# Hybrid attention and mLSTM step: the first group's output projection joins the last scan, the other groups' mLSTM halves join their attention halves, and w_out is held as float16 pairs

## The chip, the cores and the metric

One core of one Trainium2 chip runs the kernel. The metric is the device time of one execution in microseconds (us), as the median of the runs shown. The engines are named as in the profile: PE (TensorE matmul), PEld (its weight loads), DVE (VectorE), ACT (ScalarE), POOL (GpSimd), SP (the queue that issues most transfers).

## The reference

One layer: adaLN modulations from the conditioning, an input projection, attention beside a bidirectional mLSTM, one output projection over both, then a SwiGLU feed-forward layer. All inputs and outputs are float32.

```python
h = rmsnorm(x, norm1_w) * (1 + sc1) + sh1
aq, ak, av, mq, mk, mv, mo, mg = jnp.split(h @ w_in, SPLIT_POINTS, axis=-1)
...
attn_o = attention(aq, keys, vals)
...
hm, st_f, st_b = mlstm_bidir(heads(mq), heads(mk) * (MLSTM_DK ** -0.5), heads(mv), gates, init_f, init_b)
hm = rmsnorm(hm.transpose(0, 2, 1, 3), mlstm_norm_w.reshape(MLSTM_HEADS, MLSTM_DV))
hm = (hm.reshape(B, T, MLSTM_WIDTH) * jax.nn.sigmoid(mo.astype(F32))).astype(x.dtype)
mix = jnp.concatenate([attn_o, hm], axis=-1) @ w_out
x = x + g1 * mix
h2 = rmsnorm(x, norm2_w) * (1 + sc2) + sh2
x = x + g2 * swiglu(h2, w_gu, w_down)
```

D_MODEL is 1024, the attention and mLSTM widths are 512 each, D_FF is 2816. There are 128 context tokens and 1024 latent tokens, so 1152 rows.

## The kernel before

The 1152 rows are nine blocks of 128 (`NB`), block 0 the context, in three groups of three blocks (`CB`, `CT` = 384 columns). Float32 accuracy is kept by splitting every operand into a high and a low part and adding three products: high by high, high by low, low by high. The parts are fp32r (feed-forward, scores, output projection) or float16 (input projection, attention values).

The stages, in the order of the program:

1. Front: modulations from `w_ada` (`ada_rest`, L417, whose units load 512 KB and issue eight `strip_products`), normalisation, keys, values and gates, then queries. Four chunks of the modulations are made here; the sixth (`ns` = 5, the second gate) is left for stage 3.
2. Projection of the four mLSTM heads, one after another (`head_project`, L743), woven with the scan of the head before (`head_mlstm`, L825) and with the attention of group 0 (`attention`, L994). `Scaled` (L179) loads raw weights, finds their power-of-two scale with ACT, and `pairs` (L211) makes float16 pairs in the four `ipair` buffers.
3. The scan of the last head, woven by yields with `ada_rest((5,), ...)` at 0.5, the attention half of group 0's output projection (`attn_out_first`, L1208) at 0.35 and the attention of group 1 at 0.14. Group 0's sum goes to DRAM (`x1a_d`), and so does every head's `hm` (`hm_d`, token-major).
4. `prefill` (L1152): for all nine blocks the mLSTM half of the output projection: `hm` is loaded, transposed on PE, split in two, multiplied with the lower half of `w_out`, gated, added to x. Groups 0 and 1 keep their sums in `x1`; group 2's go to DRAM (`x1_d`). `norm2` (L1282) of group 0 follows in the same loop. The loop gives the attention of group 1 0.35 steps per yield.
5. The feed-forward layer of groups 0, 1, 2 (`groups`, `gate_up` L1319, `down` L1342). Beside group c goes the attention of group c+1; when that ends, `attn_out` (L1254) adds its attention half to x1, with the upper half of `w_out` loaded anew for each of groups 1 and 2.

Tile's planner orders the instructions of each engine with a timeline of its own, by program order and by the raised priority of blocks under `hot(n)`; each engine then executes its instructions strictly in that order. A pool that is opened where another was closed takes its memory tile by tile: each new tile waits for the last readers of what lay there. `beside` and `weave` (L902, L62) advance side generators by fractions of a step per yield of the main one.

PSUM is eight banks: three for the scores `S`, and during stages 2 and 3 three `mm` and two `wi`; from stage 4 on four `mm` and one `po`.

Of the kernel before, what the change touches and what calls it, by code (L numbers as in the profile page):

```python
# [8 lines left out]
F32 = mybir.dt.float32  # L9
# [31 lines left out]
CSB = 21  # L41
SINGLES = [(b,) for b in range(NB)]
# [3 lines left out]
def hybrid_step(ctx: ExitStack, tc: tile.TileContext, I: dict, O: dict):  # L46
# [49 lines left out]
    cp = ctx.enter_context(tc.tile_pool(name="cp", bufs=1, reuse_waits="tile"))  # L96
    es_wp = ExitStack()
# [9 lines left out]
    hm_d = [drp.tile([CT, 512], F32, name=f"hm_d{c}") for c in range(NCH)]  # L107
    g_d = drp.tile([2, 2, D], F32, name="g_d")
    x1a_d = [drp.tile([P, D], F32, name=f"x1a_d{i}") for i in range(CB)]
    x1_d = [drp.tile([P, D], F32, name=f"x1_d{i}") for i in range(CB)]  # L110
# [68 lines left out]
    class Scaled:  # L179
# [31 lines left out]
        def pairs(self, dve_every=2):  # L211
            out = []
            n, b = self.n, self.shape[1]
            for j, raw in enumerate(self.raws):
                w = wp.tile([P, 2, 1024], F16, name=nm("ipair"), tag="ipair", bufs=4)
                hi, lo = w[:, 0, :n], w[:, 1, :n]
# [17 lines left out]
    ncol = cp.tile([P, 16], F32, name="ncol")  # L234
    vsc = cp.tile([P, 4], F32, name="vsc")

# [10 lines left out]
    gp = es1.enter_context(tc.tile_pool(name="gp", bufs=1, reuse_waits="tile"))  # L247
    QT = gp.tile([P, 4, P], F32, name="QT")
# [210 lines left out]
    ada = ada_rest((2, 4, 3), padded_sil(adp.tile([P, KD, 32], F32, name="silp2")),  # L459
# [11 lines left out]
    next(steps)  # L471

# [38 lines left out]
    for c in range(NCH):  # L511
        with hot(100):
            features(c)
        prods = linear_tok(kvg_pairs, 0, 272, evac_kvg, (tuple(range(c * CB, c * CB + CB)),), bank if c == 1 else bankA)
        if c > 0:
            weave(prods, chain(steps, ada), KD, 10)
# [8 lines left out]
    mlp = es1.enter_context(tc.tile_pool(name="mlp", bufs=1, reuse_waits="tile"))  # L525
    mwh = mlp.tile([P, 512], F32, name="mwh")
    for tag, shape, bufs, dt in (("cs", [P, P + 1], CSB, F32), ("c0f", [P, P + 1], 2, F32), ("c0b", [P, P + 1], 1, F32), ("hm", [P, NB, P], 2, F32), ("ssh", [P, NB], 2, F32), ("nu", [P, 2, P + 1], 4, F32),
                                 ("it", [P, 2, P + 1], 3, F32), ("dn", [P, 2], 3, F32), ("jkh", [P, P], 1, BF16), ("sd", [P, 2, P], 4, F32),
                                 ("dt", [P, 2, P], 4, F32), ("so", [P, P], 9, F32), ("va", [P, P + 1], 9, F32), ("kT", [P, P], 9, F32),
# [205 lines left out]
    dve.tensor_scalar(out=mwh, in0=mwh, scalar1=0.5, scalar2=None, op0=ALU.mult)  # L735
# [4 lines left out]

    MB = 9

    def head_project(h, st):  # L743
# [4 lines left out]
        nxt_steps = groups_in[h + 2].ready() if h + 1 < NH else iter(())  # L748
        next(nxt_steps, None)
        st["q"] = [None] * NCH  # L750
        st["b"] = [None] * NB

        def evac(b, ps):
# [15 lines left out]
            update(b, kt, va)  # L769

# [54 lines left out]
    def head_mlstm(h, st):  # L825
# [7 lines left out]
        hm = mlp.tile([P, NB, P], F32, name=nm("hm"), tag="hm", bufs=2)  # L833
# [6 lines left out]
        def weights(b):  # L840
            qTb = st["q"][b // CB][:, b % CB * P : (b % CB + 1) * P]
            pd = bank()
            mm(pd[:, 0:P], blocks[b][0], qTb, start=True, stop=True)
            r = b * 4 + h
            mm(pd[:, P : 3 * P], identb, maskb.rearrange("p d l -> p (d l)"), start=True, stop=False)
            mm(pd[:, P : 3 * P], selb[:, r : r + 1].to_broadcast([P, P]), NM3.rearrange("p d l -> p (d l)"), start=False, stop=True)
            dt = mlp.tile([P, 2, P], F32, name=nm("dt"), tag="dt", bufs=4)
            for d in range(2):
                act(dt[:, d], pd[:, (d + 1) * P : (d + 2) * P], AF.Exp, bias=qcol(0, d, b, h))
            sd = mlp.tile([P, 2, P], F32, name=nm("sd"), tag="sd", bufs=4)  # L850
            dve.tensor_tensor(out=sd, in0=bc(pd[:, 0:P], 1, [P, 2, P]), in1=dt, op=ALU.mult)
            return qTb, sd
# [3 lines left out]
        for b in range(NB):  # L856
# [29 lines left out]
            act(hm[:, b, :], nu[:, 0, 0:P], AF.Copy, scale=dn[:, 0:1])  # L886
            dve.scalar_tensor_tensor(out=hm[:, b, :], in0=nu[:, 1, 0:P], scalar=dn[:, 1:2], in1=hm[:, b, :], op0=ALU.mult, op1=ALU.add)
            jk = mlp.tile([P, P], BF16, name=nm("jkh"), tag="jkh", bufs=1)
            act(jk, hm[:, b, :], AF.Square, accum_out=ssh[:, b : b + 1])
            pool.tensor_tensor(out=hm[:, b, :], in0=hm[:, b, :], in1=so, op=ALU.mult)  # L890
            if b in ends:
                b0 = ends[b]
                n = b + 1 - b0
                v = hm[:, b0 : b + 1, :]
                r = rsqrt(mlp, ssh[:, b0 : b + 1], n, 1.0 / P)
                pool.tensor_tensor(out=v, in0=v, in1=bc(r, 2, [P, n, P]), op=ALU.mult)
                for c in range(b0 // CB, b // CB + 1):
                    (nc.scalar.dma_start if h == NH - 1 and c > 0 else dma)(hm_d[c][:, h * P : (h + 1) * P].rearrange("(b p) n -> p b n", p=P), hm[:, c * CB : (c + 1) * CB, :])
# [35 lines left out]
    big = [hp.tile([P, KD * CT], F32R, name=f"kst{kv}", tag=f"b{kv}") for kv in range(NKV)]  # L934
    kst = [t[:, 0 : 2 * (NB + 1) * P].rearrange("p (t n) -> p t n", t=2) for t in big]
    mix_spare = [t[:, 2 * (NB + 1) * P :].rearrange("p (k x) -> p k x", k=4) for t in big]
# [611 lines left out]
```

## Time and profile before

| what | us |
|---|---|
| runs shown, median of 3 | 1571.77 |
| lowest and highest of them | 1571.01, 1575.17 |
| the profiled execution | 1574.08 |
| its span, first to last instruction | 1572.3 |

| engine | busy us | share of the span |
|---|---|---|
| PE | 1487.7 | 95% |
| PEld | 1247.3 | 79% |
| DVE | 1022.9 | 65% |
| ACT | 771.8 | 49% |
| POOL | 271.4 | 17% |

A PE record lasts longer than the distance to the next one, because matmuls are pipelined; so what a matmul costs is read from the distance between two starts, not from its duration. A view by stages gives for each stretch of the span the busy time of each engine, the number of its instructions in brackets, the granted clock of PE (1.00 is full) and the transfers. A view by groups gives busy time and mean duration, and behind the second bar the idle time just before these instructions, with what ended it.

### The profile page before, as it was taken

To read this page: it belongs to the slowest core of one execution; us is meant where nothing else is said; L and a number is where in the kernel's file an instruction comes from. 1 tells how busy PE (TensorE), PEld (TensorE's weight loads), DVE (VectorE), ACT (ScalarE), POOL (GpSimd) and SP (SyncE) were. 2 spreads that over 40 slices of the span, in tenths; PEclk is the share of its full clock that TensorE was granted. 3 is DMA by queue.
4 is the path that set the end of the run, shared out by engine and by line. 5 is a ranking of instruction groups with operands and counts; after the bars stand their busy time and mean duration, and the time that the engine had idled before them with its cause. 6 is when DMAs were issued, how large, how long until landed. Compare 5 with 4: busy or idle time off the path is not lost.

```text
span 1572.3 us, 23397 instructions
## 1 busy us (share of the span) xinstructions
PE 1487.7 (95%) x8539; PEld 1247.3 (79%) x8539; DVE 1022.9 (65%) x2025; ACT 771.8 (49%) x1409; POOL 271.4 (17%) x357
## 2 busy tenths in 40 slices
PE   6899999999999689999999999999999999999996
PEld 3544567676766468898998989989898989999995
DVE  4878554737659576677555677877866585554555
ACT  4754465847656344545432444556552443323332
POOL 0213333322343242100110101000010101001111
PEclk9899999999999799999999999999999999999998
DMA  9664323523556847767555447878763545544441
GB/s 360 186 182 157 97 68 41 121 47 68 114 150 162 265 80 197 184 174 175 154 154 149 147 126 236 195 170 180 179 162 114 168 133 168 161 130 138 143 139 54
DMA packets 387881, 236.91 MB, mean 151 GB/s; under 512 B 170198, under 2 KB 346790, under 8 KB 387766
## 3 DMA queue, kind: packets, MB, share of 16 engines
q1 hardware_dynamic: 385110, 231.84, 54.1%
q10 hardware_dynamic: 2656, 3.58, 1.1%
q8 instruction: 67, 1.10, 0.3%
q14 instruction: 48, 0.39, 0.1%
HBM read 183.79 MB, written 13.26 MB: 125 GB/s over the span
## 4 chain that ended last, share of the span: by engine, by line
PE 77%; DVE 11%; DMA 5%; ACT 4%; issue 2%; SPq 0%; POOL 0%; ACTq 0%; DVEq 0%; POOLq 0%
PE mm L1316 11%; PE mm L1317 11%; PE mm L1315 11%; PE mm L1115 5%; PE mm L1116 5%; PE mm L1117 5%; PE S L1035 3%; PE wi L483 3%; PE wi L485 3%; PE wi L484 3%; PE mm L116 2%; PE mm L1147 1%; PE mm L1148 1%; PE mm L1149 1%; PE po L1060 1%
## 5 line engine op out<-in xcount | busy, mean ns | idle before, releaser
L152 ACT CAST whi<-raw 128x1024 fp32r<-128x1024 f32 (+1 forms) x216 | 222.3, 1029 | 411.0 <-PE mm L1316 156.5
L137 DVE TENSOR_TENSOR wlo<-raw,whi 128x1024 fp32r<-128x1024 f32 (+1 forms) x216 | 260.4, 1206 | 202.9 <-ACT whi L152 202.3
L1316 PE MATMUL mm<-aTl,whi 128*128 128x384 f32 x1056 | 355.7, 337 | 2.7 <-DVE aTl L137 2.7
L1317 PE MATMUL mm<-aTh,wlo 128*128 128x384 f32 x1056 | 354.3, 336 | 0.0
L1315 PE MATMUL mm<-aTh,whi 128*128 128x384 f32 x1056 | 353.3, 336 | 0.0
L137 POOL TENSOR_TENSOR hl<-tn,hl 128x384 fp32r<-128x384 f32 x66 | 84.4, 1279 | 840.0 <-ACT hl L1338 748.3
L1316 PEld LDWEIGHTS mm<-aTl,whi 128*128 128x128 f32 x1056 | 198.5, 188 | 3.9 <-DVE aTl L137 3.3
L1315 PEld LDWEIGHTS mm<-aTh,whi 128*128 128x128 f32 x1056 | 198.1, 188 | 0.6
L1317 PEld LDWEIGHTS mm<-aTh,wlo 128*128 128x128 f32 x1056 | 198.4, 188 | 0.0
L1116 PE MATMUL mm<-wlo,hl 128*128 128x512 f32 x372 | 145.7, 392 | 0.0
L1115 PE MATMUL mm<-whi,hl 128*128 128x512 f32 x372 | 144.3, 392 | 0.0
L1117 PE MATMUL mm<-whi,hl 128*128 128x512 f32 x372 | 143.4, 392 | 0.0
L483 PE MATMUL wi<-ipair,hT 128*128 128x384 f16 (+2 forms) x408 | 135.6, 335 | 1.7 <-ACT hT L507 1.2
L484 PE MATMUL wi<-ipair,hT 128*128 128x384 f16 (+2 forms) x408 | 135.6, 335 | 0.0
L485 PE MATMUL wi<-ipair,hT 128*128 128x384 f16 (+2 forms) x408 | 132.1, 335 | 1.0 <-DVE hT L137 1.0
L1042 DVE SCALAR_TENSOR_TENSOR pl<-pr,st,ph 128x1152 f16<-128x1152 f32 (+1 forms) x72 | 96.0, 1333 | 31.7 <-ACT ph L1041 31.4
L1037 DVE TENSOR_REDUCE st<-S 128x1 f32<-128x1152 f32 (+1 forms) x72 | 88.9, 1235 | 16.3 <-PE S L1035 16.1
L1038 ACT ACTIVATE pr<-S,st 128x1152 f32<-128x1152 f32 (+1 forms) x72 | 81.3, 1130 | 32.4 <-DVE st L1037 29.3
L1041 ACT ACTIVATE ph<-pr,st 128x1152 f16<-128x1152 f32 (+1 forms) x72 | 83.9, 1165 | 23.8 <-DVE st L1040 6.7
L1035 PE MATMUL S<-kst,qT 128*128 128x384 f32 (+1 forms) x400 | 87.6, 349 | 4.8 <-ACT pr L1038 4.8
L1104 DVE TENSOR_TENSOR t<-mm,gl 128x512 f32<-128x512 f32 x102 | 69.1, 687 | 26.2 <-DMA gl<-g_d 11.5
L1117 PEld LDWEIGHTS mm<-whi,hl 128*128 128x128 f32 x372 | 69.9, 188 | 14.2
(375 smaller groups left out, 2538.4 us busy)
## 6 DMA issues: line engine op xcount, KB each, us to landing
raw<-in_w_gu_dram SPq DMA_DIRECT2D x132, 512.0 KB
raw<-in_w_down_dram SPq DMA_DIRECT2D x60, 512.0 KB
a<-in_w_ada_dram SPq DMA_DIRECT2D x24, 512.0 KB
gl<-g_d SPq DMA_DIRECT2D x36, 256.0 KB
aw<-in_w_ada_dram SPq DMA_DIRECT2D x16, 512.0 KB
iraw<-in_w_in_dram SPq DMA_DIRECT2D x32, 256.0 KB
raw<-in_w_out_dram SPq DMA_DIRECT2D x12, 512.0 KB
x<-in_x_sample_dram SPq DMA_DIRECT2D x11, 512.0 KB
```

The lines of the kernel that those rows point to most:

```text
L137: (dve if eng == "dve" else pool).tensor_tensor(out=out, in0=full, in1=hi, op=ALU.subtract)
L152: nc.scalar.copy(hi[:, :n], raw[:, :n])
L483: mm(ps[:, :n], ah, wh[:, k % 2, c0 : c0 + n], start=(k == 0), stop=False)
L484: mm(ps[:, :n], ah, wl[:, k % 2, c0 : c0 + n], start=False, stop=False)
L485: mm(ps[:, :n], al, wh[:, k % 2, c0 : c0 + n], start=False, stop=(k == KD - 1))
L1035: mm(S[:, n, 0:w], qT[:, h, :], kst[kv][:, t, c0 + n * w : c0 + (n + 1) * w], start=(t == 0), stop=(t == 1))
L1115: mm(ps, ah, wh[:, k % 2, :], start=(k == 0), stop=False)
L1116: mm(ps, ah, wl[:, k % 2, :], start=False, stop=False)
L1117: mm(ps, al, wh[:, k % 2, :], start=False, stop=(k == nk - 1))
L1315: mm(ps, wh[:, k, :], th[:, k, :], start=(k == 0), stop=False)
L1316: mm(ps, wh[:, k, :], tl[:, k, :], start=False, stop=False)
L1317: mm(ps, wl[:, k, :], th[:, k, :], start=False, stop=(k == KD - 1))
```

## The change

The stage `prefill` is gone, with `x1a_d`, `x1_d` and `load_x1`.

- `head_mlstm` transposes its own `hm` on PE when a group of blocks ends, splits it into float16 high and low and writes that to `hm_d`, already feature-major. Group 0's last head goes straight into `mx0`; its other three heads are loaded from `hm_d`.
- `w_o[0]`, the upper half of `w_out`, is loaded and scaled once during the last head's projection; its pairs take the four `ipair` buffers, now in a pool `wq` that lives to the end, and serve all three groups. `w_o[1]`, the lower half, is loaded in the last scan for group 0, and again by `out_pieces` for groups 1 and 2.
- `first_out`, woven with the last scan at 0.8, does both halves of group 0. Its sum stays in SBUF, and `norm2` of group 0 reads it there, with one step of group 1's attention after each of its six yields.
- `attn_out` of groups 1 and 2 does both halves: 48 matmuls a block in place of 24, with `hm_d` loaded as ready operands.
- The last modulation chunk (5) moves into the front, whose side rates go from 1.15 to 1.5 and from 10 to 12.
- The score weights of the last head (`scan_weights`, formerly inside the scan) are made in its projection.
- The pools of the feed-forward stage open after the last scan, on the right side, where the scan's pool lay; x1 of groups 1 and 2 is loaded from the input.

```diff
-    ada = ada_rest((2, 4, 3), padded_sil(adp.tile([P, KD, 32], F32, name="silp2")),
+    ada = ada_rest((2, 4, 3, 5), padded_sil(adp.tile([P, KD, 32], F32, name="silp2")),
...
+    w_o = [Scaled([[(full_view, out_rows(half, n, j))] for n in range(2) for j in range(2)], (2, 512)) for half in range(2)]
+    groups_in.append(w_o[0])
...
             update(b, kt, va)
+            if h == NH - 1:
+                st["w"][b] = scan_weights(h, st, b)
...
                 for c in range(b0 // CB, b // CB + 1):
-                    (nc.scalar.dma_start if h == NH - 1 and c > 0 else dma)(hm_d[c][:, h * P : (h + 1) * P].rearrange("(b p) n -> p b n", p=P), hm[:, c * CB : (c + 1) * CB, :])
+                    v = hms[c]
+                    pool.tensor_tensor(out=v, in0=v, in1=bc(r[:, c * CB - b0 : (c + 1) * CB - b0], 2, [P, CB, P]), op=ALU.mult)
+                    ps = bank()
+                    for i in range(CB):
+                        transpose(ps[:, i * P : (i + 1) * P], v[:, i])
+                    psv = ps[:, 0:CT].rearrange("p (b x) -> p b x", b=CB)
...
+                    nc.scalar.copy(t[:, :, 0], psv)
+                    sub(t[:, :, 1], psv, t[:, :, 0], "dve")
+                    if own is not None and c == 0:
+                        ends_done.add(c)
+                        continue
...
-    weave(linear_tok(w_q, 0, 512, evac_q(qp, qcc, qss, qw)), beside((gates, 0.7), (ada, 1.15), (kwork, 0.6), (steps, 0.3)), 40, 40)
+    weave(linear_tok(w_q, 0, 512, evac_q(qp, qcc, qss, qw)), beside((gates, 0.7), (ada, 1.5), (kwork, 0.6), (steps, 0.3)), 40, 40)
...
+    def first_out(oT, ready, mx, hm_done):
...
+        steps = w_o[1].ready()
+        next(steps)
...
+        def block(half, i):
             for n in range(2):
...
+                ps = out_block(w_o[half].made, n, mx[:, half, i])
+                v = x1[:, i, cs]
+                tmp = gt[:, 4 + n]
+                dve.scalar_tensor_tensor(out=tmp, in0=ps, scalar=wos[:, half : half + 1], in1=gt[:, 2 * n + (i > 0)], op0=ALU.mult, op1=ALU.mult)
+                (pool if half == 0 else dve).tensor_tensor(out=v, in0=v, in1=tmp, op=ALU.add)
                 yield
+        for i in range(CB):
+            while i not in ready:
                 yield
+            attn_pair(mx[:, 0, i], oT[i], "dve")
+            next(steps, None)
+            yield
+            for _ in block(0, i):
+                next(steps, None)
+                yield
+        emit(steps)
...
+        w_o[1].made = w_o[1].pairs(homes=homes)
+        keep_scale(1)
+        yield
+        while 0 not in hm_done:
+            yield
+        for i in range(CB):
+            yield from block(1, i)
...
+    def attn_out(c, a, oT, gs):
+
+        pieces = (w_o[0].made, out_pieces())
...
+                dma(m[1].rearrange("p k t x -> p (k t x)"), hm_d[c][i * P : (i + 1) * P, :])
+                attn_pair(m[0], oT[i], "dve")
+            for half in range(2):
+                for n in range(2):
+                    ps = out_block(pieces[half], n, m[half])
+                    with hot(200):
+                        cs = slice(n * 512, (n + 1) * 512)
+                        t = t2()
+                        dve.scalar_tensor_tensor(out=t, in0=ps, scalar=wos[:, half : half + 1], in1=gs[n], op0=ALU.mult, op1=ALU.mult)
+                        dve.tensor_tensor(out=x1[i][:, cs], in0=x1[i][:, cs], in1=t, op=ALU.add)
...
-    weave(scan, beside((ada, 0.5), (first, 0.35), (att, 0.14)), 37, 37)
+    weave(scan, beside((first, 0.8), (att, 0.14)), 37, 37)
     while len(done) < CB:
         next(att)
+    emit(scan)
     emit(first)
...
+    cur["x1"] = new_x1(0)
+    cur["x1n"] = x1s
+    with hot(400):
+        cur["rs"] = stats(x1s)
+    for i in range(CB):
+        dma(cur["x1"][i], x1s[i])
+        for _ in norm2(0, cur, i):
+            next(att, None)
     es1.close()
     es_wp.close()
     es_d.close()
```

More of the change, by code (lines that the diff above doesn't have):

```diff
@@ L840, in weights @@
         def weights(b):
[L841 to L852, printed above, removed]
+            return st["w"].pop(b) if alone else scan_weights(h, st, b)
         ahead = [weights(b) for b in range(depth)]
@@ L1121, in three_blocks, with out_pieces @@
                 done(i, ps)
[L1123 to L1124 removed]
+    def out_pieces():
+        out = []
         for n in range(2):
[L1126 removed]
             for j in range(2):
[L1128 to L1133 removed]
+                raw = wp.tile([P, 1024], F32, name=nm("raw"), tag="raw", bufs=2)
+                w = wp.tile([P, 2, 1024], F16, name=nm("wo"), tag="whi", bufs=5)
+                dma(raw.rearrange("p (a b) -> p a b", b=512), out_rows(1, n, j))
+                hi, lo = w[:, 0], w[:, 1]
+                act(hi, raw, AF.Copy, scale=wos[:, 2:3])
+                dve.scalar_tensor_tensor(out=lo, in0=raw, scalar=wos[:, 2:3], in1=hi, op0=ALU.mult, op1=ALU.subtract)
+                out.append(tuple(v.rearrange("p (a b) -> p a b", b=512) for v in (hi, lo)))
+        return out
     def out_gates():
```

288 lines of the change are left out of this document (121 added, 167 removed).

## The prediction

> **What bounds the kernel now.** I read the view by stages first, cut where the trace changes character: the end of the head projections (458), the last scan (to 515), the prefill stage (to the first gate-up matmul, 615), the feed-forward layer.
>
> ```profile
> core 0: us, PE busy (x) PEld busy (x) DVE busy (x) ACT busy (x) POOL busy (x), PEclk, DMA share, GB/s
> 100.00:165.00 65.00, 59.39 (x374) 27.88 (x374) 49.94 (x175) 31.89 (x57) 16.65 (x11) 0.97 0.51 158
> 165.00:458.00 293.00, 285.91 (x1851) 203.43 (x1850) 167.15 (x441) 183.08 (x513) 97.41 (x212) 0.98 0.37 82
> 458.00:515.00 57.00, 49.95 (x312) 37.35 (x313) 52.18 (x140) 35.04 (x89) 22.54 (x23) 0.96 0.66 170
> 515.00:615.00 100.00, 77.99 (x383) 61.42 (x381) 64.37 (x134) 45.20 (x67) 30.96 (x24) 0.92 0.62 166
> 615.00:1552.00 937.00, 932.19 (x5093) 864.19 (x5092) 602.52 (x855) 406.02 (x530) 87.47 (x68) 1.00 0.59 159
> ```
>
> PE is full in the projections (286 of 293 us) and in the feed-forward layer (932 of 937, clock 1.00). In the last scan it is DVE that is full: 52.2 of 57 us, 92%. In the prefill stage nothing is full. Its start is in the chain of waits: a weight load, then the first `hm` load, before PE does anything:
>
> ```profile
> 514.53 5.16 DMA raw<-in_w_out_dram
> 522.46 4.25 DMA t<-hm_d
> ```
>
> The price of a matmul is the distance of starts. Three pairs from the order of PE in time, then a stretch that begins with a low clock:
>
> ```profile
> 616.55 0.33 PE L1315 MATMUL mm<-aTh,whi 128*128 128x384 f32 x1
> 616.72 0.33 PE L1316 MATMUL mm<-aTl,whi 128*128 128x384 f32 x1
> 857.45 0.40 PE L1147 MATMUL mm<-whi,mx 128*128 128x512 f32 x1
> 857.69 0.39 PE L1148 MATMUL mm<-wlo,mx 128*128 128x512 f32 x1
> 123.99 0.38 PE L484 MATMUL wi<-ipair,hT 128*128 128x512 f16 x1
> 124.20 0.38 PE L485 MATMUL wi<-ipair,hT 128*128 128x512 f16 x1
> 526.75 1.12 PE L116 MATMUL mm<-ident,t 128*128 128x128 f32 x4 [9.40 <-DMA t<-hm_d]
> ...
> 529.56 0.63 PE L1147 MATMUL mm<-whi,mx 128*128 128x512 f32 x1
> 529.99 0.63 PE L1148 MATMUL mm<-wlo,mx 128*128 128x512 f32 x1
> ...
> 534.83 0.40 PE L1147 MATMUL mm<-whi,mx 128*128 128x512 f32 x1
> ```
>
> So a 512-wide fp32r product costs 0.23 us, a float16 one 0.215, and at the low clock 0.43, until 534.8.
>
> The kernel is two PE-bound stages with a DVE-bound stage and a latency-bound one between them. The change removes the last of these and puts its work into the other three.
>
> **The change part by part.**
>
> *Feed-forward layer.* Groups 1 and 2 get 2 x 3 x 24 = 144 mLSTM products of 0.215 us: +31. Their 144 attention products go from 0.23 to 0.215: -2. PE is full there, so this is time, **+29** (bounds 27 and 36: the upper one if the gap of 0.23 stays and the first `hm` load of 4.25 us shows). The `hm` loads for blocks 0 and 1 of a group have homes that are free early, the one for block 2 waits for block 0's 48 products and has block 1's 48 x 0.215 = 10 us to land; the weight loads behind it on SP wait for the pieces of `attn_out` anyway.
>
> *Attention of group 1.* Its score products by stage, six to a head, and two of the value products:
>
> ```profile
> 458.00:515.00 57.00, 7.73 (x36) 0.96 0.66 170
> 515.00:615.00 100.00, 8.09 (x36) 0.92 0.62 166
> 615.00:1552.00 937.00, 45.37 (x216) 1.00 0.59 159
> 428.10 0.27 PE L1059 MATMUL mm<-phT,vs 128*128 128x256 f16 x1
> 428.21 0.27 PE L1060 MATMUL mm<-plT,vs 128*128 128x256 f16 x1
> ```
>
> Six heads ran in the last scan and six in the prefill stage, whose 33 yields at 0.35 gave 11 steps. Now there are six steps in `norm2`, so some three heads fewer. Each costs the full stage 6 x 0.17 + 9 x 0.11 = 2 us: **+6** (0 to 12, the latter if none is done in `norm2`).
>
> *Projections.* Scans of heads 0 to 2 gain 27 transposes and the last projection nine score weights of four products each; the small products lie 0.11 us apart as those above: 27 x 0.11 + 36 x 0.11 = 7. PE had 7 us without work there: **+6** (0 to 7).
>
> *Front.* The 64 strips of the last chunk come here. They have this row from the last scan, sixteen in one microsecond:
>
> ```profile
> 464.49 1.07 PE L341 MATMUL mm<-ip,gta 128*32 128x256 f32 x16
> 103.82 14.47 SPq L423 DMA_DIRECT2D a<-in_w_ada_dram x5
> ```
>
> That is 4 us on a PE that is 91% busy from 100 to 165, plus 4 MB through three `a4` buffers, on a queue that already waits there (five issues took 14.5 us, as SP stands until a buffer is free, with `iraw` and `q_d` behind it). The transfers have room (share 0.51). I take **+6**, from 0 (hidden in the PE gaps) to 20 (eight loads at the pace of these five, 2.9 us each, of which nothing but 3 us hides).
>
> *The last scan.* DVE is the bound, so I count DVE. What goes and what stays, from the groups of DVE between 458 and 515:
>
> ```profile
> L1246 DVE TENSOR_TENSOR gta<-mm,gta 128x512 f32<-128x512 f32 x6 | 4.1, 682 | 1.2 <-POOL hm L890 1.2
> L851 DVE TENSOR_TENSOR sd<-mm,dt 128x256 f32<-128x256 f32 x9 | 3.8, 418 | 0.7 <-ACT dt L849 0.5 <-PE wi L866 0.2
> L137 DVE TENSOR_TENSOR ir<-ir,ip 128x1024 fp32r<-128x1024 f32 x3 | 3.7, 1228 | 2.9 <-ACT ip L152 2.9
> L451 DVE TENSOR_TENSOR ir<-mm,ir 2x512 f32<-2x512 f32 x2 | 1.3, 672 | 0.0
> L453 DVE TENSOR_SCALAR ir<-ir 2x512 f32<-2x512 f32 x2 | 0.8, 400 | 0.0
> ```
>
> Gone: the gate products (4.1), the score weights (3.8), the fp32r splits (3.7), the modulation rows (2.1), 13.7 in all. What comes has these rows elsewhere in the run:
>
> ```profile
> L219 DVE SCALAR_TENSOR_TENSOR ipair<-iraw,isc,ipair 128x1024 f16<-128x1024 f32 x10 | 13.1, 1307 | 5.5 <-ACT ipair L218 5.5
> L137 DVE TENSOR_TENSOR ipair<-iraw,ipair 128x1024 f16<-128x1024 f32 x10 | 13.7, 1369 | 1.8 <-ACT ipair L222 1.8
> L1105 DVE TENSOR_TENSOR x<-x,t 128x512 f32<-128x512 f32 x102 | 71.4, 711 | 0.9
> L1104 DVE TENSOR_TENSOR t<-mm,gl 128x512 f32<-128x512 f32 x102 | 69.1, 687 | 26.2 <-DMA gl<-g_d 11.5 <-PE mm L1393 6.5 <-PE mm L1117 5.4
> L137 DVE TENSOR_TENSOR hT<-full,hT 128x384 f16<-128x384 f32 x24 | 13.9, 611 | 0.0
> ```
>
> Pairs of both halves of w_out, 2 x (2 x 1.31 + 2 x 1.37) = 10.7 (`w_o[0]`'s cannot be earlier, since its four buffers hold the last head's weights to the end of the projection); twelve gated products at 0.7 = 8.4; six adds, on DVE for the mLSTM half, 6 x 0.71 = 4.3; three splits of the attention output 2.1; the splits of `hm` for two heads, 6 x 0.6 = 3.6: 29.1. So 52.2 - 13.7 + 29.1 = 67.6 us of DVE, at its 92% 74 us instead of 57: **+17** (+3, if the pairs and 4 us more slip into its holes, to +38, at a DVE that is 72% busy). PE has less to do there than DVE: 144 x 0.215 = 31, scan, transposes and attention some 20 more.
>
> *The prefill stage.* Its 100 us go. In their place stands, between the end of the scan and the first gate-up product, `norm2` of group 0 for three blocks, which needs squares, one rsqrt, then ACT, PE, ACT/DVE, ACT, POOL in a row. Its work on ACT before: the square, y and the last cast of block 0, and the last cast of block 2, with out blocks and attention in between:
>
> ```profile
> 539.22 1.06 ACT L1278 ACTIVATE jk<-x 128x1024 bf16<-128x1024 f32 x1 [1.07 <-POOL x L1105]
> ...
> 544.64 1.34 ACT L1294 ACTIVATE y<-x,ry 128x512 f32<-128x512 f32 x2 [1.35 <-DVE ry L133]
> ...
> 551.20 0.62 ACT L1309 CAST aTh<-fl 128x512 fp32r<-128x512 f32 x1
> ...
> 575.88 0.63 ACT L1309 CAST aTh<-fl 128x512 fp32r<-128x512 f32 x1
> ```
>
> One block takes 5.4 us from its square to y and 7 from y to aTh; from the first y to the last cast the three took 32, as they waited for their sums. Now they are ready together and overlap: 5.4 and 7 for the first, some 3.5 of ACT's own (1.34, twice 0.62, two smaller ones) for each other, two squares more: **21** (14, if the squares hide under the scan and ACT alone counts, to 32). The first weight pieces can be loaded under this, as their buffers are those of w_o[1], free after group 0's last product. So 100 becomes 21, **-79** (-86 to -68).
>
> *Clock.* PE idles in that tail, and the feed-forward layer then starts on a low clock. After its 9.4 us of idling before 526.75 PE needed 0.43 us a product up to 534.8, that is 8 us at half rate, 4 lost. With transposes and scores in the tail I take **+2** (0 to 4). The Trainium skill, TensorE: Matmul & The Clock Gate, Part 1, says that the clock halves after some 3.4 us without work and needs as long under work; by that page the loss would be 1.7 us where the row shows 4, and the sum would not move by more than that.
>
> *Sum.* 29 + 6 + 6 + 6 + 17 - 79 + 2 = -13. The profiled execution took 1574.1 us (span 1572.3, 1.8 around it), 2.3 over the median; it goes to 1561, and the median of runs, 1571.8, to **1559**. A difference within 0.3%, 5 us, is about what a measurement of this kernel can't tell from none. Put as a date: the feed-forward layer gets 35 us longer, so the change gains only if it starts before 615 - 35 - 2 = 578; I expect 565.
>
> **The rivals.**
>
> *DVE's order decides and it stalls (slower).* The last scan's DVE queue is in order; behind each pair or gate product that waits stand the small operations of the scan (dn, nu) and the attention's reductions, and ACT, POOL and PE wait for these. New waits enter: w_o[1]'s loads come only when `w_o[0]`'s pairs have freed the raw buffers, then eight passes of ACT, a scale through PE, the pairs. If DVE is busy for 72% as in a stage with many waits (the prefill stage shows 64%, the front 77%), the scan takes 67.6 / 0.72 = 94, +38 instead of +17, and `norm2` runs at its upper bound, +11 more: -13 + 21 + 11 = +19, **1591**. It decides from a first gate-up product after 583. For it: the queue is nearly full already. Against it: in this same stage the planner kept DVE at 92%.
>
> *DVE takes the work in its holes (faster).* Before 458 DVE is not full (167 of 293 us), and head 2's splits can go there; ops stretched by POOL shrink as the sums leave POOL. Scan +3 instead of +17, tail 14 instead of 21: -13 - 14 - 7 = -34, **1538**. Against it: `w_o[0]`'s pairs are pinned behind the last projection.
>
> *The front pays for the modulation (no change).* At its upper bound, +20 instead of +6: +1, **1573**. For it: SP already stands on the `a4` buffers. Against it: share of transfers 0.51.
>
> **How the numbers follow.** Forecast 0.45 (of which 0.41 is faster and 0.04 within 0.3%), stalled DVE 0.22, holes 0.20, front 0.13 (0.02 faster, 0.06 same, 0.05 slower). So faster 0.63, same 0.10, slower 0.27. The forecast's own range is 1548 to 1570. Adding the two outer cases to within 1 in 10 each gives 1536 to 1592; the bounds of all terms at once, -56 and +49, would be wider, but they won't all go one way.
>
> **What would show it.** Right: the first gate-up product near 565 of the new span; 937 + 35 = 972 us from there to the last group's end, with PE as full as before; DVE over 90% from 470 to 545; the head projections' end near 470. Wrong: DVE under 80% in the last scan, or gate-up after 578; gaps of PE in the two `attn_out`; a front that is over 10 us longer. If the feed-forward stage grows by much less than 35 us, my price for the moved products is wrong, since nothing there can hide them.

## The result, and the profile after

The changed kernel takes 1598.23 us (median of 4 runs, 1595.83 to 1600.49) beside 1572.76 us of the kernel before on the same chip: 1.0161 times, with a 95% interval of 1.0138 to 1.0183. It is slower by 25 us where I had forecast 13 us faster, and it lies above the range. The profiled execution has a span of 1593.8 us, 21.5 more than before.

The view by stages of the changed kernel, core 0, cut where the head projections begin and end, where the last scan operation of ACT (L912) starts, after the last output product of group 0, and at the first gate-up product:

```profile
core 0: us, PE busy (x) PEld busy (x) DVE busy (x) ACT busy (x) POOL busy (x), PEclk, DMA share, GB/s
100.00:185.10 85.10, 72.69 (x455) 33.80 (x454) 64.97 (x215) 40.07 (x76) 23.83 (x15) 0.86 0.61 191
185.10:485.30 300.20, 287.19 (x1843) 201.63 (x1842) 158.56 (x420) 183.41 (x518) 84.73 (x200) 0.99 0.34 74
485.30:556.50 71.20, 54.65 (x279) 37.38 (x279) 54.74 (x147) 42.57 (x113) 22.88 (x32) 0.86 0.35 84
556.50:567.00 10.50, 10.50 (x51) 4.77 (x49) 8.50 (x32) 0.80 (x3) 2.11 (x3) 1.00 0.00 1
567.00:595.40 28.40, 12.59 (x79) 10.23 (x77) 16.82 (x45) 19.94 (x35) 5.97 (x5) 0.82 0.75 218
595.40:1572.00 976.60, 973.44 (x5316) 877.90 (x5317) 637.84 (x909) 422.59 (x556) 84.83 (x68) 1.00 0.60 156
```

The head projections of the kernel before, in the same view with their exact ends:

```profile
165.00:453.10 288.10, 282.34 (x1825) 200.63 (x1825) 164.68 (x433) 178.72 (x501) 94.02 (x207) 0.98 0.37 81
```

With the kernel before cut in the same way (165.0, 453.1, last scan operation 512.9, first gate-up product 615.0, end 1572.3), the 21.5 us fall apart like this. The prediction's terms for the scan and for the prefill stage have to be taken together, since I had cut at other events:

| stretch | before | after | difference | predicted |
|---|---|---|---|---|
| to the first head product | 165.0 | 185.1 | +20 | +6 |
| head projections | 288.1 | 300.2 | +12 | +6 |
| their end to the first gate-up product | 161.9 | 110.1 | -52 | 17 - 79 = -62 |
| feed-forward layer to the end | 957.3 | 998.4 | +41 | 29 + 6 + 2 = +37 |

Every row is worse than predicted, and none by an accident of one place. The stage that was to go did go: 162 us became 110. What the change pays for that elsewhere is 73 us and not 49.

In the order of PE in time, the end of the front. The last three rows are the first head products:

```profile
156.49 0.38 PE L497 MATMUL wi<-ipair,hT 128*128 128x512 f16 x1
161.46 1.71 PE L352 MATMUL mm<-strip_sel,part 128*128 128x2 f32 x8 [4.59 <-ACT part L446]
163.09 2.79 PE L346 MATMUL mm<-a,silp 128*32 128x256 f32 x24
...
181.38 1.87 PE L455 MATMUL mm<-part,strip_sel 128*2 128x512 f32 x2 [0.70 <-ACT part L446]
...
185.07 0.48 PE L827 MATMUL wi<-hT,ipair 128*128 128x384 f16 x1
185.34 0.53 PE L828 MATMUL wi<-hT,ipair 128*128 128x384 f16 x1
185.66 0.53 PE L829 MATMUL wi<-hT,ipair 128*128 128x384 f16 x1
```

The q projection ends at 156.9, earlier than before (161.2), but 28 us of modulation strips, copies, rows and gate work stand behind it, at a granted clock of 0.58 (157.0 to 185.1). The first head products still start 0.32 us apart; in the kernel before they start 0.16 us apart.

The same view between the last head product and the first output product:

```profile
485.13 0.33 PE L497 MATMUL wi<-ipair,hT 128*128 128x384 f16 x1
...
502.74 1.26 PE L116 MATMUL mm<-ident,hmc 128*128 128x128 f32 x4 [6.54 <-POOL hmc L923]
...
508.38 0.30 PE L116 MATMUL mm<-ident,kt 128*128 128x128 f32 x1 [0.63 <-DVE oT L1104]
...
509.86 0.38 PE L1189 MATMUL mm<-ipair,mx 128*128 128x512 f16 x1
```

PE stands for 6.5 us at the transposes of head 2's `hm`, which wait for POOL's scaling. Queued behind them is the `kt` transpose of the last block: its product was done at 485, ACT had written `kt` by 489, and PE transposes it at 508. The last scan cannot start before it.

And the end of that stretch, PE first and then ACT:

```profile
566.76 0.38 PE L1191 MATMUL mm<-iw,mx 128*128 128x512 f16 x1
566.97 0.82 PE L116 MATMUL mm<-ident,hmc 128*128 128x128 f32 x6
576.52 1.11 PE L116 MATMUL mm<-ident,y 128*128 128x128 f32 x4 [8.73 <-ACT y L1300]
...
595.45 0.69 PE L1321 MATMUL mm<-aTh,whi 128*128 128x384 f32 x1 [5.05 <-ACT whi L152]
```

```profile
567.50 0.86 ACT L932 CAST hmT<-mm 128x384 f16<-128x384 f32 x2 [9.73 <-PE mm L116]
...
570.12 1.06 ACT L1284 ACTIVATE jk<-x1a 128x1024 bf16<-128x1024 f32 x1 [1.76 <-DVE hmT L137]
...
575.75 1.33 ACT L1300 ACTIVATE y<-x1a,ry 128x512 f32<-128x512 f32 x2 [2.41 <-DVE ry L133]
...
593.83 0.62 ACT L1315 CAST aTh<-fl 128x512 fp32r<-128x512 f32 x1 [1.86 <-DVE fl L1310]
```

The output products run 10 us past the last scan operation, and only then do the squares, the rsqrt and `norm2` start, 28 us in a row.

### The profile page after: what moved, and what is told of

Read it like the earlier page. It is cut to its first block, busy times and chain, and to the rows that moved or that the text cites. A ratio compares the mean times of both kernels' runs of the same rounds, so it can differ in the third digit from the quotient of the medians.

```text
span 1593.8 us, 23426 instructions
## 1 busy us (share of the span) xinstructions
PE 1494.4 (94%) x8545; PEld 1217.9 (76%) x8545; DVE 1028.1 (65%) x2047; ACT 777.6 (49%) x1448; POOL 240.9 (15%) x341
## 4 chain that ended last, share of the span: by engine, by line
PE 58%; DVE 3%; DMA 1%; ACT 0%; issue 0%; ACTq 0%
PE mm L1322 12%; PE mm L1323 12%; PE mm L1321 11%; PE mm L1155 5%; PE mm L1156 5%; PE mm L1157 4%; PE S L1075 3%; PE po L1100 1%; PE po L1099 1%; PE mm L1189 1%; PE mm L1190 1%; PE mm L1191 1%; DVE fl L1310 1%; DVE x L1145 1%; DMA plT<-pl 1%; DVE wlo L137 0%
## 5 line engine op out<-in xcount | busy, mean ns | idle before, releaser
L152 ACT CAST whi<-raw 128x1024 fp32r<-128x1024 f32 (+1 forms) x204 | 209.0, 1025 | 375.6 <-PE mm L1322 151.5
L137 DVE TENSOR_TENSOR wlo<-raw,whi 128x1024 fp32r<-128x1024 f32 (+1 forms) x204 | 245.4, 1203 | 171.4 <-ACT whi L152 168.8
L1157 PEld LDWEIGHTS mm<-whi,hl 128*128 128x128 f32 x372 | 69.9, 188 | 14.4
L1155 PEld LDWEIGHTS mm<-whi,hl 128*128 128x128 f32 x372 | 69.9, 188 | 13.8
```

Of the source, the lines that this page charges most:

```text
L137: (dve if eng == "dve" else pool).tensor_tensor(out=out, in0=full, in1=hi, op=ALU.subtract)
L152: nc.scalar.copy(hi[:, :n], raw[:, :n])
L1155: mm(ps, ah, wh[:, k % 2, :], start=(k == 0), stop=False)
L1157: mm(ps, al, wh[:, k % 2, :], start=False, stop=(k == nk - 1))
```

## The experiments

All ratios are against the kernel before, with their 95% intervals; the changed kernel itself stands at 1.0161. The kernel before was timed again beside each batch of runs, with medians from 1571.1 to 1573.6 us, so differences between runs of two batches are good to some 2 us.

### The front alone

Run b_front5 gives the kernel before this one part of the change; run a_no5 takes it out of the changed kernel.

```diff
-    ada = ada_rest((2, 4, 3), padded_sil(...
+    ada = ada_rest((2, 4, 3, 5), padded_sil(...
...
-beside((gates, 0.7), (ada, 1.15), ...
+beside((gates, 0.7), (ada, 1.5), ...
...
-        return out(), ada
+        return out(), iter(())
```

> The kernel before with one part of the change alone: the last modulation chunk (64 strips, 4 MB) is computed in the front beside the q projection and no longer beside the last scan. Theory (the front pays in full): the head projections start at 180 to 187 of the span instead of 165, the last scan gets at most 5 us shorter in return (2 us of DVE rows, 16 strips of PE), so 1583 to 1593 us. Rival (the front is late for another reason, such as a different order from the rest of the change): start at 165 to 171, time 1568 to 1578.

> The changed kernel without the last modulation chunk: its strips are left out, the rows of chunk 2 are written into its place, so that two small stores take the place of 64 strips and 4 MB. Theory: head projections start at 163 to 167 and everything behind moves up by the same 18 to 22 us, 1576 to 1581 us in all. Rival (another stage absorbs it, since the last scan waits for something fixed such as w_out's loads): 1588 to 1598.

b_front5: 1592.28 us, 1.012 (1.010 to 1.014), first head product at 183.6; the last scan gave nothing back. a_no5: 1579.68 us, 1.0038 (1.0027 to 1.0049), first head product at 165.1. Both came out as their theories said, and both say the same: chunk 5 in the front costs 18 to 19 us, and everything behind moves with it.

### What in the front costs them

Three edits to the changed kernel: the last chunk's loads left out, the q stores on ACT's queue, the modulation woven in faster.

```diff
+            if n == 5 and kept:
+                return kept[-1]
...
-                    dma(q_d[bb], ...
+                    nc.scalar.dma_start(q_d[bb], ...
...
-beside((gates, 0.7), (ada, 1.5), ...
+beside((gates, 0.7), (ada, 2.2), ...
```

> The changed kernel with the last chunk's 64 strips, their copies and rows all there, but without its 4 MB of loads: the strips read the last tile of chunk 3 again, so that the gate of the feed-forward layer is a wrong one. Theory (the loads pay: they stand in SP's order and three buffers): head projections start at 165 to 171 instead of 185, 1578 to 1585 us. Rival (the strips, the copies on ACT and the rows on DVE pay): they start at 178 to 186, 1591 to 1598.

> The changed kernel with the nine stores of q to memory on ACT's queue instead of SP's. Theory (in SP's order the strips' loads stand behind stores of q that wait for DVE and POOL; 124.7, 140.2 and 148.4 were the three places): loads run on, last strip near 165 to 170 instead of 180, head projections 10 to 15 us earlier, 1583 to 1589 us. Rival A (the three buffers of the strips pace the loads, and PE's order frees them): nothing gained, 1594 to 1600. Rival B (ACT stands at the stores' waits in SP's stead, and PE waits for ACT): slower, over 1602.

> The changed kernel with the modulation's steps woven in faster beside the q projection (2.2 for 1.5, and 14 for 12 beside the one before), so that its chain is due before the projection's end. Theory (it is lateness: the last units stand behind the q projection, and the head projections wait for the last row's sum on DVE, which frees the PSUM banks): head projections start at 165 to 174 instead of 185, 1578 to 1588 us. Rival (the front is full, on PE and DVE, whatever the order): start at 180 to 187, 1594 to 1600.

No theory held. Without the 4 MB of loads: 1598.04 us, 1.0161 (1.0138 to 1.0184), first head product at 181.6, so 16.5 of the 20 us stay, as the rival said; and the 3.5 us gained are lost again by the end of the last scan (563.1 instead of 556.5). Stores on ACT: 1603.23 us, 1.0192 (1.0174 to 1.0210), the number of rival B; but PE's waits for ACT's copies of the strips (L446) grow only from 6.6 to 7.7 us. Woven in faster: 1606.99 us, 1.023 (1.0198 to 1.0262), and the first head product at 190.8, later still. What comes last differs. Without the loads PE's wait before the first head product is for the modulation's last row on DVE:

```profile
181.56 0.48 PE L830 MATMUL wi<-hT,ipair 128*128 128x384 f16 x1 [4.28 <-DVE row L459]
```

With the faster weave that row is done by 178.7. PE then stands at two transposes of the gate work, which wait for ACT. The third line is the end of this front by stages:

```profile
183.00 0.48 PE L116 MATMUL mm<-ident,qw__1808 128*128 128x128 f32 x1 [2.95 <-ACT qw__1808 L650]
188.72 0.48 PE L116 MATMUL mm<-ident,qi__1809 128*128 128x128 f32 x1 [5.25 <-ACT qi__1809 L651]
165.00:191.00 26.00, 10.16 (x48) 5.28 (x48) 24.75 (x54) 21.14 (x41) 2.63 (x2) 0.63 0.47 143
```

DVE is busy there for 24.75 of 26 us and ACT for 21, while PE has 10. So most of it is not the transfers, and an earlier place in the weave only moves the wait to other work: the end of the front has more for DVE and ACT to do than fits under the q projection. Chunk 5 itself brings little of that: in the changed kernel its rows are 3.3 us of DVE and its two copies 1.1 us of ACT, out of 23.9 and 17.2 between 157 and 185.1; the rest is mostly key stacks, weight pairs and the q normalisation. Why so small an addition makes the front 20 us longer is not shown; no run took DVE's or ACT's work out, or gave the strips more than the one `part` and the one `row` buffer that they have.

### The feed-forward layer

```diff
-            for half in range(2):
+            for half in range(1):
```

> The changed kernel without the 144 mLSTM products and their gated adds in the output projections of groups 1 and 2 (loads and pairs stay), so that part is missing from the output. Theory (PE is full there, each product is 0.215 us of time): the feed-forward stage gets 30 to 32 us shorter, 1565 to 1569 us in all. Rival (the pieces of w_out, the hm loads or the adds pace the projections, products lie partly under them): 10 to 25 us shorter, 1573 to 1588.

a_noml: 1567.94 us, 0.9969 (0.9957 to 0.9982). From the first gate-up product to the last it takes 936.8 us instead of 968.4: 31.6 us for 144 products, 0.219 each. The price was right.

### Between the scan and the first gate-up product

Run a_noh1 drops the loop `for i in range(CB): yield from block(1, i)`. The other two:

```diff
-        for _ in norm2(0, cur, i):
-            next(att, None)
+        emit(norm2(0, cur, i))
...
-    weave(scan, beside((first, 0.8), (att, 0.14)), 37, 37)
     while len(done) < CB:
         next(att)
+    weave(scan, beside((first, 0.8),), 37, 37)
```

In the last one the weave also moves behind the loop that ends the attention of group 0, so that the rest of that attention is emitted ahead of the scan.

> The changed kernel without the 72 mLSTM products and gated adds of group 0 (the pairs of w_out's second half and the transposes stay), so that part is missing from the output. They ran from 551 to 567, while the last scan operation on ACT is at 556.5. Theory (they are the last thing before norm2, and no longer have a scan to lie beside): the first gate-up product comes 9 to 13 us earlier, 1585 to 1589 us. Rival (norm2's start is set by the last hm split on ACT and DVE, with the products in its shadow): 0 to 4 us earlier, 1594 to 1598.

> The changed kernel with no attention steps woven into norm2 of group 0; they run in the feed-forward layer. Theory (the two to three heads in that stage stand on ACT and DVE between norm2's own operations: each 1.2 + 1.25 us on ACT and 1.35 + 1.4 on DVE): the stretch from the last out product to the first gate-up product shrinks from 28 to 18 to 22 us, the feed-forward layer grows by 2 us a head, 4 to 6, so 1592 to 1597 us in all. Rival (the chain of norm2 itself sets it, attention lies beside it): 28 stays 26 to 28, time 1600 to 1605.

> The changed kernel with no attention heads of group 1 beside the last scan; five heads go to the feed-forward layer. Theory (DVE's in-order queue: each head puts 1.35 and 1.4 us operations between the scan's small ones, and a Newton step of rsqrt or a denominator stands behind them): the scan and what hangs on it end 12 to 20 us earlier, the feed-forward layer grows by 10, so 1588 to 1597 us. Rival (the scan is its own chain or PE's order of out products): the end moves by under 5 us, 1603 to 1608.

a_noh1: 1591.53 us, 1.0113 (1.0098 to 1.0129), first gate-up product 5.8 us earlier. That is between the two theories: of the 10 us of products past the scan about half is paid, the rest lies beside the last `hm` splits. a_noatt: from the last output product to the first gate-up product 23.9 instead of 28.7 us, between the theory's 18 to 22 and the rival's 26 to 28; over the run that is 1595.06 us, 1.0139 (1.0114 to 1.0165), whose interval overlaps the changed kernel's. a_att0: the last scan operation comes 19 us earlier (537.7), so the heads do stretch the scan (by their rows five heads are some 14 us of DVE); but the first gate-up product comes at 596.6, 1 us later, and the time is 1597.56 us, 1.0159 (1.0140 to 1.0179). The six attention steps of `norm2` now begin with group 1's first heads, and five sets of score products stand between the last output product and the first gate-up product instead of two. What was taken from the scan was handed to the stage behind it.

### The head projections

Run a_sw computes the last head's score weights in the scan again; run a_rawhm leaves out the transposes and splits of `hm` of heads 0 to 2.

```diff
-            if h == NH - 1:
-                st["w"][b] = scan_weights(h, st, b)
...
-            return st["w"].pop(b) if alone else scan_weights(h, st, b)
+            return scan_weights(h, st, b)
```

```diff
+                    if h < NH - 1:
+                        t = mlp.tile([P, CB, 2, P], F16, name=nm("hmT"), tag="hmT", bufs=2)
+                        nc.scalar.copy(t[:, :, 0], v)
+                        for k in range(2):
+                            dma(hm_d[c][...], t[:, :, 0])
+                        yield
+                        continue
                     ps = bank()
```

> The changed kernel with the last head's score weights back in its scan, three blocks ahead as before. Theory (the four small products and the exp and DVE work of each block stretch the last projection, whose queue waits on ACT and DVE): head projections 4 to 8 us shorter, of which the scan gives back at most half: 1592 to 1597 us. Rival (the projection's 12 us come from the hm transposes and splits of heads 0 to 2): projections unchanged within 2 us, scan longer by the 3.8 us of DVE, 1598 to 1604.

> The changed kernel without the 27 hm transposes and the nine splits on DVE of heads 0 to 2 (a float16 copy of the untransposed hm is stored twice, so that group 0 to 2 get a wrong mLSTM half). Theory (these, with PSUM banks and DVE behind them, are what makes the last two head projections 6 and 8 us longer): projections 286 to 293 us instead of 300, 1586 to 1592 us in all. Rival (something else, such as the place of the scan in the weave): 297 to 302, 1595 to 1600.

a_sw: 1594.59 us, 1.0139 (1.0124 to 1.0154), projections 300.1 us, unchanged: the score weights do not lengthen them. The scan grows by 4 us, as the rival said. The time is in the theory's range all the same, but its interval overlaps the changed kernel's, and the first gate-up product comes no earlier (596.2). a_rawhm: 1576.25 us, 1.0027 (1.0015 to 1.0040), 22 us less (21 by the ratios). Its first two stages:

```profile
183.60:472.30 288.70, 282.21 (x1826) 200.50 (x1825) 154.79 (x414) 184.10 (x519) 87.50 (x200) 0.99 0.38 77
472.30:535.00 62.70, 52.37 (x271) 35.94 (x271) 51.71 (x145) 42.75 (x114) 22.90 (x32) 0.89 0.38 96
```

The projections are back at 288.7 us, and from their end to the first gate-up product (574.2) it is 101.9 instead of 110.1. PE's busy time falls by 5 us only; 6.5 us are idle time that is gone, for the most part where the changed kernel waits for `qT` on DVE (4.1 us in all at the starts of the last two heads) and for ACT. The first of these waits (at 323.6) ends before the first transpose of `hm` (330.9), so at least that one is not a queue standing behind a transpose: the planner also puts the engines' instructions in another order when the transposes are there. The run does not separate the two. What it takes out costs as much as chunk 5 in the front, within the scatter of the batches, and the time saved is larger than the expectation allowed.

### Versions

v1 emits group 0's mLSTM half, squares and `norm2` block by block; v2 adds chunk 5 in the first head's projection, v3 also the score weights in the scan. v4 has the faster weave of a_rate2, squares by block and no attention in `norm2`; v4sw has the score weights in the scan too.

> The changed kernel with group 0's mLSTM half, its sum of squares and its norm2 emitted block by block after the scan, and no attention in norm2. Theory (the 39 us from the scan's last operation to the first gate-up product are 10 of products, 23 of norm2's chain and 5 of attention, one after the other): with norm2 of block 0 and 1 beside the products of block 1 and 2, 12 to 20 us earlier, the feed-forward layer 2 to 4 longer: 1581 to 1590 us. Rival (what is late next sets it: the first weights of the feed-forward layer on SP, behind x and hm): 0 to 6 us, 1592 to 1598.

> v1 with the last modulation chunk out of the front and into the first head's projection, in eight loads of 128 columns through a buffer that is idle there. Theory (PE is full there, so 64 strips of half the width and eight small products cost 4 to 6 us, and SP and the buffers have nothing else to do): 12 to 16 us less than v1, 1566 to 1577 us. Rival (the strips' loads hold SP ahead of the next head's weights): no better than v1.

> v2 with the last head's score weights back in the scan. Theory: 2 to 5 us less than v2, as between the changed kernel and the run with this edit alone, so 1562 to 1574 us. Rival (in a scan that is shorter now they lie on its path): 0 to 4 us more than v2.

> The changed kernel with the faster modulation, the sum of squares of each block of group 0 by itself, and no attention in norm2. Theory (the parts add up: front 10 to 18, attention 3, squares and rsqrt of two blocks beside the products 2 to 4): 1572 to 1583 us. Rival (the planner's new order gives it back, as it did when norm2 was emitted block by block): 1590 to 1605.

> v4 with the last head's score weights back in the scan: 2 to 5 us less than v4 by the run with that edit alone, 1568 to 1580 us. Rival (the weights now stand between the out products in PE's order): 0 to 4 us more than v4.

None reached the time that its theory gave. v1 took 1615.22 us, 1.0273 (1.0244 to 1.0302): the planner put each block's transposes ahead of the next block's products, and PE's queue is in order:

```profile
575.22 1.97 PE L116 MATMUL mm<-ident,y 128*128 128x128 f32 x8 [5.90 <-ACT y L1297]
589.40 1.97 PE L116 MATMUL mm<-ident,y 128*128 128x128 f32 x8 [5.82 <-ACT y L1297]
```

v2 took 1618.36 us, 1.0287 (1.0257 to 1.0318): its front ends at 167.4, but the first head's projection grows to 69.5 us (55.3 in the changed kernel), 7.1 of it at one wait of PE for the strips' load. v3: 1614.20 us, 1.0267 (1.0244 to 1.0290), the 4 us under v2 that were expected of its edit. v4: 1602.98 us, 1.0195 (1.0163 to 1.0227), 4 us better than a_rate2, whose front it has. v4sw: 1592.09 us, 1.0126 (1.0097 to 1.0156). So the score weights' place is worth 11 us here (4 of them in the projections, 8 from there to the last scan operation) and 4 in v3 and a_sw: what the same edit is worth hangs on what stands beside it.

v5 keeps the transposes and moves them off PE. Each chunk of heads 0 to 2 is split first (ACT and POOL) and transposed on the DMA queue; the score weights are back in the scan, and `norm2` has no attention. The score weights' buffers go back to those of the kernel before (`dt` four for two, `sd` four for nine). v6 also moves chunk 5 to `norm2` of group 0 and the first gate-up products.

```diff
+                    if not alone:
+                        t = mlp.tile([P, CB, 2, P], F16, name=nm("hmU"), tag="hmU", bufs=2)
+                        nc.scalar.copy(t[:, :, 0], v)
+                        sub(t[:, :, 1], v, t[:, :, 0], "pool")
+                        tt = mlp.tile([P, CB, 2, P], F16, name=nm("hmT"), tag="hmT", bufs=2)
+                        nc.sync.dma_start_transpose(tt..., t...)
+                        dma(hm_d[c][...], tt...)
+                        yield
+                        continue
```

> The changed kernel with hm of heads 0 to 2 split before it is transposed, on ACT and POOL, and transposed by DMA instead of PE, ACT and DVE; score weights back in the scan; no attention in norm2. Theory (hm's way through PE, PSUM and DVE holds the projections and the scan's start): projections 287 to 293 us long, 1568 to 1579 us in all. Rival (any way to transpose costs it, SP now stands at POOL's splits with the weights behind it): 1588 to 1600.

> v5 with the last modulation chunk neither in the front nor in the last scan: eight loads of 128 columns through an idle buffer, five of them beside norm2 of group 0 and three beside the first gate-up products. Theory (front back to 165, and 64 strips beside a stage where PE idles): 8 to 16 us less than v5, 1555 to 1568 us, faster than both kernels. Rival (the strips' loads and rows lie on norm2's chain or hold the first weights): within 4 us of v5 or more.

v5: 1570.96 us, 0.9995 (0.9985 to 1.0004), the same as the kernel before and 27 us under the changed kernel; the two small edits had given 3 to 4 us each alone. Against the changed kernel the projections are 12.5 us shorter, the way from there to the last scan operation is as long (71.0 us), and from that to the first gate-up product it takes 29 us instead of 39: the last output product starts at 539, ahead of the last scan operation (544.8). Its view by stages, the projections and from there to the last scan operation:

```profile
186.30:474.00 287.70, 282.21 (x1802) 198.75 (x1801) 154.99 (x409) 181.34 (x507) 93.28 (x206) 0.97 0.42 82
474.00:545.00 71.00, 60.55 (x344) 39.05 (x343) 63.91 (x170) 46.56 (x126) 26.82 (x36) 0.96 0.41 93
```

And the instructions that write the split tile or read it, with their shortest, median and longest time in ns, first and last start in us:

```profile
L924 ACT CAST hmU<-hmc x9: 495/512/521, 329.4 to 497.3; 128x384 f16<-128x384 f32 x9
L137 POOL TENSOR_TENSOR hmU<-hmc,hmU x9: 903/954/1775, 331.9 to 497.9; 128x384 f16<-128x384 f32 x9
L927 SPq DMA_TRANSPOSE hmT<-hmU x9: 1211/1230/1302, 332.8 to 501.0; - x9
```

So in the projections it is not the transposing as such that costs, but its way through PE, a PSUM bank, ACT and DVE: with the transposes on SP they are as short as without any (288.7 in a_rawhm), and PE is busy again for just what it was before (282 us). For the scan this is not shown: a_rawhm's takes 62.7 us and v5's 71.0, but v5 has the score weights in it. No run has the DMA transposes alone.

v6: 1579.83 us, 1.0048 (1.0034 to 1.0063). Its front ends at 164.4 and its projections at 452.4, as early as in the kernel before, but from the last scan operation (524.1) to the first gate-up product it takes 52 us, where v5 takes 29. With a single buffer for the strips, PE stands at three of the loads with `norm2`'s transposes behind it:

```profile
550.10 1.08 PE L346 MATMUL mm<-spare,t 128*32 128x128 f32 x16 [2.03 <-DMA spare<-in_w_ada_dram]
...
558.65 1.08 PE L346 MATMUL mm<-spare,t 128*32 128x128 f32 x16 [5.46 <-DMA spare<-in_w_ada_dram]
```

No version that ran beats both kernels. By the dates of the first head product (186.3 in v5, 164.4 in v6), a version with v6's front and v5's end would be some 20 us faster; that is an estimate, and where chunk 5 would go in it wasn't tried.

## Why the prediction was wrong

It failed not by one step but by four of its seven terms, all in the same direction, and by one way of pricing that three of them share.

*Projections, +6 (0 to 7): measured +12, and some 21 with what it causes behind.* This step and the front failed most. I charged 27 transposes and 36 score-weight products at 0.11 us of PE, and six DVE splits to the last scan. Run a_rawhm shows that the transposes and splits of heads 0 to 2 alone cost 21 to 22 us. They were priced as slots on a PE with 7 us free. In truth each chunk is a chain POOL, PE, ACT, DVE through four queues. The clearest price of that is at the end: PE stands 6.5 us for POOL at 502.7, with the last block's `kt` behind it, ready at 489 and transposed at 508. How the 12 us inside the projections divide between such waits and the planner's other order stays open. The score weights, the other half of this term, do not lengthen the projections here (a_sw).

*Front, +6 (0 to 20): measured +20.* I had the size as the upper bound and as the rival "the front pays for the modulation", but that bound rested on SP and three buffers, and without the loads 16.5 us stay. I had counted 4 us of PE, and of ACT and DVE nothing, though DVE was busy there for 50 of 65 us. What failed is the overlap: the front's end has the gates, the key stacks and the pairs on ACT and DVE too, and the head projections wait for whichever of these is last. Why that comes to 20 us stays open.

*norm2 tail, 21: measured 39 from the last scan operation.* The chain itself was well sized: 23.9 us without attention. What I left out is that the output products need not end with the scan; 10 us run past it, and half of that is paid (a_noh1). The attention steps add 5 (a_noatt); I had counted only on the heads they do, not on the operations they put between `norm2`'s own on ACT and DVE.

*Last scan, +17 (74 us): measured 71 us from the projections' end.* The length was nearly right, the reason was not. DVE is busy for 54.7 of 71.2 us, 77%, under the 80% that I had named as the sign that the view is wrong. My sum had 67.6 us of DVE. What the traces show is a stage with a late start (the `kt` at 508) in which no engine is full. Without the heads it ends 19 us earlier (a_att0), so DVE's work counts in it, but that run does not separate work from order. In v5, with the score weights back in the scan, DVE is busy for 63.9 of 71.0 us, 90%. Two bounds of this term don't follow from their own working: 67.6 less 14.7 at 92% is 57.5, so +0.5 and not +3, and 94 is +37 and not +38.

*Attention of group 1, +6: some 10 by count.* The groups of PE in the feed-forward layer:

```profile
L1075 PE MATMUL S<-kst,qT 128*128 128x384 f32 x246 | 51.7, 346 | 0.1
L1099 PE MATMUL po<-phT,vs 128*128 128x256 f16 x198 | 46.7, 275 | 0.0
```

246 score products instead of 216 are five heads more, not three, at the 2 us each that I had priced.

*Right:* the feed-forward products, 31.6 us where I had 31. With 2 us less for float16, 10 for the heads and the low clock at its start (granted 0.50 for 6.6 us, 595.4 to 602.0, so some 3 us lost where I had 2) that makes the layer's 41 to within 2. Right too was the date as a measure. I wrote that the change gains only if the first gate-up product comes before 578: it came at 595.4, 17 us after, and with 4 us more in the feed-forward layer that is the 21.5 us of the span. Of the rivals, "DVE's order decides and it stalls" names the sign and the late date, but its place, a scan of 94 us, was not where the time went, and its 1591 us lies below the result. The forecast charged each stage only what its busiest engine would do, and the bounds were drawn around that; so the range ended at 1592, below the result.

## What to carry to other kernels

A step that is moved beside other work can cost several times its slots on the busiest engine (here some 21 us for 3 us of transposes): list the queues that its chain crosses, and at each of them what stands behind the waiting instruction. Where a chain crosses PE and PSUM only to change a layout, try the DMA queue first. And relief in one stage counts only if nothing is poured from it into the next: take the date at which the next stage starts, not the length of one, as the measure.

## What was not expected of the hardware

The nine DMA transposes of 128x768 float16 elements in v5 landed 4.1 us after issue (the median) and cost no time that shows in the projections, though the attention's own transposes share the queue. The Trainium skill, DMA: Bandwidth & Descriptors, DMA Transpose (X-bar), allows this path for two-byte types with a destination in SBUF, which is why v5 splits `hm` before it transposes; the rows of `hmU` and `hmT` above are of that kind. It warns of two transposing streams from different queues in flight at once; all of v5's come from SP, so no run here shows that. A split on POOL took 0.954 us for 128x384 elements, nearly twice the 0.512 us of ACT's cast beside it, and POOL had room for it: it is busy for 93 of the 288 us of v5's projections.
